# Attention gates of four units moved into the Strassen pairs ahead of attention

## The chip, the cores and the metric

The kernel runs on one core of one Trainium2 chip. The metric is the device time of one execution in microseconds (us); three executions of the kernel before took 1938.79 to 1944.55 us, with a median of 1942.8 us. The engines are TensorE (PE in the profile; its weight loads are PEld), VectorE (DVE), ScalarE (ACT), GpSimd (POOL) and SyncE (SP, which here only issues DMAs).

## The reference

One layer of a hybrid trunk is applied to a prompt of 1024 tokens and to 8 samples of 16 tokens, 1152 tokens in all, with D_MODEL = 1024. One projection feeds everything; only what matters here is kept:

```python
proj = h @ w_in        # columns: q | k | v | z_att | z_ssd | x,B,C | dt | gates
q, k, v, z_att, z_ssd, xbc, dt_raw, gates = jnp.split(proj, IN_SPLITS, axis=-1)
q = rms_norm(q, q_norm_g); k = rms_norm(k, k_norm_g)          # per head of 64
o_att = attn_fn(q, k, v)                                      # chunk band with a bias by distance
att_branch = (o_att * jax.nn.silu(z_att)) @ w_att_proj
...                                                           # SSD branch: y * silu(z_ssd), grouped norm
merged = sigmoid(g_att) * att_branch + sigmoid(g_ssd) * ssd_branch
out = x + gate * (merged @ w_out)
```

The change is about `silu(z_att)`: 1024 columns, that is 8 blocks of 128, one block for each attention unit of two heads.

## The kernel before, in words

Activations lie with channels on partitions, so a block of 128 output columns of the projection is a 128 x 1152 tile. Every projection is done in three fp32r products (high weight by high activation, high by low, low by high; lines 489, 490, 492). Weights are loaded as 128 x 1024 pieces in the order in which the host has packed them ("wall"), into two raw buffers, and split into high and low parts by one ScalarE and one VectorE instruction a piece (`w_split`, lines 374 and 375).

The work comes in this order. (1) Norm and modulation, and the first block: the attention gate of unit 0. (2) The blocks computed ahead (`AHEAD_BLOCKS`, 19 of them): four merge gates singly, then 14 SSD gates as seven Strassen pairs (`pairs`, line 821), then one SSD gate singly. Each result is written to DRAM (`keep_block`), the merge gates to `gate_d` and the SiLU gates to `z_d`; a pair computes two blocks in seven forms of 24 matmuls of 288 columns, where two single blocks are 144 matmuls of 384. (3) Attention, eight units. (4) The SSD branch, 16 pairs of heads, with the remaining merge gates and one SSD gate put between them (`FILL`). (5) The output projections.

One attention unit (`attention`, line 1175) is made of generators. `dense_gen` computes q, k and v token tile by token tile (`dense_tok`, lines 555 to 557: nine tiles of 24 matmuls, with PSUM buffers "d", two of them) and then the SiLU gate of the *next* unit as a plain block (`dense`, 72 matmuls; lines 489, 490, 492, evicted in lines 999 and 1000). `prelude` normalizes q and k on GpSimd (lines 1228 to 1232) in three groups of tiles and transposes them (line 1252 for the first two groups, line 1268 for the third); after the third it frees the q/k buffer. `prompt` and `sample` do the scores (1390, 1443, 1446), the softmax, the transposes of the probabilities (1311), the products with v (1334, 1470, 1480) and multiply by the gate (1395, 1486); when both are through, `done` (line 1289) writes the gated result to `att_d` and frees the buffers of gate and v. So while the tiles of unit u+1 run, the scores of unit u are worked off beside them.

Three buffers matter to the steps below. There is one q/k buffer (tag "Q"): `dense_gen` of unit u+1 waits at `walloc` until `prelude` of unit u has freed it. There are five buffers of tag "T" for gates and v. And the q/k/v weights have two slots of three pieces (`L_W3`), one for the high and one for the low part of one unit; the gate's weights lie elsewhere (`L_WA`).

The order in which the code issues instructions is set by a planner, `run` (line 1108): it steps the dense generator, adds the estimated length of each step to a clock, and steps the other generators when their planned times have come and when a credit, earned by dense work, is positive. If the dense generator has to wait for a buffer, only the others are stepped. The builder (`schedule_with_timeline_sim=True`, line 2196) may then rearrange an engine's instructions by a timeline of its own, except those marked `late`, which stay behind the one before them.

Of the kernel before, what the change touches and what calls it, by code (L numbers as in the profile page):

```python
# [7 lines left out]
F32 = mybir.dt.float32  # L8
# [4 lines left out]
P = 128  # L13
# [15 lines left out]
RW = HALO + NP + NB * (HALO + NS)  # L29
EPS = 1e-6  # L30
AHEAD = 2
NEARLY = 15
SLOTS = (('p', 1), ('p', 3), ('p', 6), ('p', 9), ('p', 11), ('p', 13), ('p', 15))
BLOCKS = [("gate", i) for i in range(4)] + [("z", p) for p in range(NPAIR)] + [("gate", i) for i in range(4, 16)]
AHEAD_BLOCKS = BLOCKS[:4 + NEARLY]
FILL = dict(zip(SLOTS, BLOCKS[4 + NEARLY:]))
NGATE = 4 + NEARLY + len(SLOTS) - NPAIR
NZ = 5
NPR = 7
TH = NT // 2  # L40
MH = TH // 2
BIG = -1e30
# [89 lines left out]
def trunk_kernel(ctx: ExitStack, tc: tile.TileContext, h):  # L132
# [188 lines left out]
    acs_d = drp.tile([32, NT], F32, name="acs_d")  # L321
    eacs_d = drp.tile([32, NT], F32, name="eacs_d")
    gate_d = drp.tile([16, P, NT], F32, name="gate_d")
    z_d = drp.tile([1 + NPAIR, P, NT], F32, name="z_d")

    def rsqrt_small(v):

# [14 lines left out]
    def job(*raw):  # L342
        jobs.append([len(parts) + i for i in range(len(raw))])
        parts.extend(raw)
# [117 lines left out]
    for i in range(NZ + 2 * NPR, nz):  # L462
        job(h["wall"][i])
    jobs_att = [len(jobs)]
    for u in range(NU - 1):
        job(*(h["wall"][nz + 4 * u + i] for i in range(3)))
        job(h["wall"][nz + 4 * u + 3])
    job(*(h["wlast"][i] for i in range(4)))
    jobs_att.append(len(jobs))
    for x in [h["wall"][i] for i in range(nz + 4 * NU - 4, 85)] + [h["watt"][i] for i in range(8)] + [h["wssd"][i] for i in range(16)] \  # L470
            + [h["wout"][i] for i in range(8)]:
        job(x)

    def dense(ops, evict, nk=KT, outs=1, last=False, wide=False, order=(0, 1, 2), other=False, third=False, wkeep=lambda x: x):

        i = widx[0]
        widx[0] += 1
        hi, lo = yield from w_wait(i)  # L480
        if len(jobs[min(i + 1, len(jobs) - 1)]) > 3:
            w_next(i, wkeep)

        def mm(ps, o, g, k, parts=(0, 1)):
            tok = slice(g * G3, (g + 1) * G3)
            wc = slice((k * outs + o) * P, (k * outs + o + 1) * P)
            kh, kl = ops[k]
            if 0 in parts:
                nc.tensor.matmul(ps, hi.r[:, wc], kh.r[:, tok], start=k == 0, stop=False)  # L489
                nc.tensor.matmul(ps, hi.r[:, wc], kl.r[:, tok], start=False, stop=False)  # L490
            if 1 in parts:
                nc.tensor.matmul(ps, lo.r[:, wc], kh.r[:, tok], start=False, stop=k == nk - 1)  # L492

        for o in range(outs):
            if wide or (last and o == outs - 1):
                if wide or other:
                    acc = [pg(G3) for _ in range(3)]
                else:
                    sp = pss.tile([P, 2, 512], F32, tag="s", name=nm("s"))
                    acc = [psd.tile([P, G3], F32, tag="d", name=nm("d")) for _ in range(2)] + [sp[:, 0, :G3]]  # L500
                for k in range(nk):
                    while len(ops) <= k:
                        blocked[0] = "operand"
                        yield None
                    for g in range(3):
                        mm(acc[g], o, g, k)
                        if k == nk - 1:
                            yield from evict(o, g, slice(g * G3, (g + 1) * G3), acc[g]) or ()
                        yield 3 * 162.5
                    if last and o == outs - 1:  # L510
                        for x in ops[k]:
                            x.free()
                    if k == 2 and o == 0:
                        w_next(i, wkeep)
                continue
            for g in order:
                if g == 2 and third:
                    ps = pg(G3)
                elif g == 2 and att_left[0] == 0:
                    ps = pss.tile([P, 2, 512], F32, tag="s", name=nm("s"))[:, 0, :G3]  # L520
                else:
                    ps = psd.tile([P, G3], F32, tag="d", name=nm("d"))
                for k in range(nk):
                    while len(ops) <= k:
                        blocked[0] = "operand"
                        yield None
                    mm(ps, o, g, k)
                    if nk == KT and g == order[-1] and k in (3, 5, 7):
                        w_over(i, k)
                    yield 3 * 162.5  # L530
                yield from evict(o, g, slice(g * G3, (g + 1) * G3), ps) or ()
                if o == 0 and (g == 0 or len(jobs[min(i + 1, len(jobs) - 1)]) > 1):
                    w_next(i, wkeep)
        w_done(i)
# [462 lines left out]
    def ev_z(z, keep=lambda x: x):  # L997
        def ev(o, g, tok, ps):
            keep(nc.scalar.activation(z.ap[:, tok], ps, AF.Tanh, scale=0.5))
            keep(nc.vector.scalar_tensor_tensor(z.ap[:, tok], z.ap[:, tok], 1.0, ps, ALU.add, ALU.mult))  # L1000
        return ev
# [8 lines left out]

    def keep_block(n, z):
        what, i = AHEAD_BLOCKS[n - 1]
        dma(gate_d[i] if what == "gate" else z_d[1 + i], z.ap)

    z = [alloc(L_VT, "T", NT)]
    w_done(0)
# [8 lines left out]
    def do(what, *x):  # L1025
        if what == "first":
            ev_z(z[0], late)(0, x[0], groups[x[0]], first[x[0]])
            if x[0] == 2:
                dma(z_d[0], z[0].ap)
                z[0].free()  # L1030
        elif what == "sum":
            t_sum(*x)
        elif what == "split":
            t_split(*x)
        else:
            o, i, c = small_ops[x[0]]
            if c is None:
                late(nc.scalar.activation(o, i, AF.Copy))
            else:
                late(nc.vector.tensor_scalar(o, i, c, None, ALU.mult))  # L1040
# [134 lines left out]
    def attention(u):  # L1175
# [4 lines left out]
        def dense_gen():  # L1180
            qk = yield from walloc(lay, "Q", 16 * P)
            if u == 0:
                turn = alloc(lay, "T", NT)
                z = zs[0] = alloc(lay, "T", NT)
                dma(z.ap, z_d[0])
                turn.free()
            v = yield from walloc(lay, big, NT)
            nb = yield from walloc(lay, "n", 84)
            st["qk"], st["v"], st["nb"] = qk, v, nb
            if u == NU - 1:  # L1190
                dts["raw"] = yield from walloc(lay, "T", NT)

            def ev(t, ps):

                while t == 8 and "turned" not in st:
                    blocked[0] = "q and k of the first tokens"
                    yield None
                c = qk.ap[:, 2 * (t % 8) * P:2 * (t % 8 + 1) * P]
                nc.scalar.activation(c, ps[:, :2 * P], AF.Copy)
                s = alloc(lay, "q", 2 * P)  # L1200
                nc.scalar.activation(s.ap, ps[:, :2 * P], AF.Square)
                nc.vector.tensor_copy(v.ap[:, t * P:(t + 1) * P], ps[:, 2 * P:NQ])
                if u == NU - 1:
                    nc.vector.tensor_copy(dts["raw"].ap[:, t * 32:(t + 1) * 32], ps[:, NQ:])
                nc.vector.tensor_reduce(nb.ap[:, 4 * t:4 * t + 4], s.ap.rearrange("p (h d) -> p h d", d=HD), mybir.AxisListType.X, ALU.add)  # L1205
                s.free()
                st["n"] = t + 1

            yield from dense_tok(ev)
            dma(h["out_v"][u], v.ap[:, 512:])  # L1210
            if u == NU - 1:
                v_phase("ssd", F32)
                v_open[0] = True
                return
            z = zs[u + 1] = yield from walloc(lay, "Z" if u + 1 == NU - 1 else "T", NT)
            yield from dense(hops, ev_z(z))

        def prelude():
            bias = []
# [392 lines left out]
        dts["t"] = clock[0] + 3000  # L1612


    ngate = [max(4, 4 + NEARLY - NPAIR)]

    def fill_dense(*slot):
        what, i = FILL[slot]
        if what == "gate":
            yield from gate_dense()  # L1620
            return

        def ev(o, g, tok, ps):
            t = yield from walloc(L_SSD, "g", G3)
            nc.scalar.activation(t.ap, ps, AF.Tanh, scale=0.5)
            nc.vector.scalar_tensor_tensor(t.ap, t.ap, 1.0, ps, ALU.add, ALU.mult)
            store(z_d[1 + i][:, tok], t.ap)
            stored(t)

        yield from dense(hops, ev)  # L1630
# [54 lines left out]
    def ssd(p):  # L1685
# [51 lines left out]
        def main():  # L1737
# [101 lines left out]
            for t in me + [xd]:  # L1839
                t.free()  # L1840
            z = alloc(lay, "T", NT)
            dma(z.ap, z_d[1 + p])
            te, tz = clock[0] + 4000, clock[0] + 6500
            yield 3500
            for j in range(3):
# [368 lines left out]
```

## Time and profile before

| | |
|---|---|
| median of three executions | 1942.8 us (1938.79 to 1944.55) |
| profiled execution, its own time | 1943.42 us |
| span of the profile | 1941.6 us |
| granted TensorE clock | 0.999 |
| TensorE busy | 1922.7 us (99%) |
| VectorE busy | 1251.5 us (64%) |
| ScalarE busy | 798.3 us (41%) |

The first number is what is compared later; the profile is of one execution. Busy time of TensorE is that of overlapping matmuls, so a stretch in which it is busy throughout is read by how many matmuls it holds, not by its busy share. Rows of the trace give a start and a length in us from the start of the span, and the line of the kernel.

### The profile page before, as it was taken

The page shows a single profiled execution, that of the slowest core. Times are in us where ns is not written, and L with a number is a line of the kernel's source. Part 1 is how long each engine was busy: PE and PEld are TensorE (multiplying, and loading weights), DVE is VectorE, ACT ScalarE, POOL GpSimd, SP SyncE. Part 2 cuts the span into 40 slices and gives each one's busy share as a digit, 9 for nine tenths or more (in the row PEclk, how much of TensorE's full clock was granted, in tenths as well). Part 3 has the DMA queues.
Part 4 walks back from the last instruction along what each step waited for, and adds up shares of the span by engine and source line. Part 5 has one row for each costly group of instructions (what it writes and reads, how often), then busy time and mean ns, then how long its engine had stood idle before and what let it go on. Part 6 is the DMA issues. An engine that isn't in the chain of part 4 may idle for free.

```text
span 1941.6 us, 35765 instructions
## 1 busy us (share of the span) xinstructions
PE 1922.7 (99%) x14259; PEld 1842.4 (95%) x14259; DVE 1251.5 (64%) x2577; ACT 798.3 (41%) x1639; POOL 339.7 (17%) x615
## 2 busy tenths in 40 slices
PE   7999999999999999999999999999999999999999
PEld 5999999999899998998999999999999999999999
DVE  6756634555556456558597988888885434777732
ACT  7533324444454444545655546465453311111200
POOL 0000003213123131221022343242241300000000
PEclk9999999999999999999999999999999999999999
DMA  8222342343333333423345354554558742331341
GB/s 316 92 81 95 109 173 69 96 129 116 97 117 101 122 116 94 130 82 115 119 132 181 132 162 152 168 173 140 160 192 289 292 144 93 105 105 56 89 143 52
DMA packets 85966, 258.73 MB, mean 133 GB/s; under 512 B 14732, under 2 KB 15768, under 8 KB 85800
## 3 DMA queue, kind: packets, MB, share of 16 engines
q1 hardware_dynamic: 77416, 229.57, 36.5%
q0 software_dynamic: 8384, 26.88, 3.6%
q8 instruction: 112, 1.84, 0.4%
q14 instruction: 54, 0.44, 0.1%
HBM read 202.72 MB, written 53.68 MB: 132 GB/s over the span
## 4 chain that ended last, share of the span: by engine, by line
PE 92%; DVE 3%; DMA 2%; ACT 1%; issue 1%; POOL 0%; SPq 0%; ACTq 0%; DVEq 0%; POOLq 0%
PE d L489 11%; PE d L492 11%; PE d L490 11%; PE d L557 5%; PE d L555 5%; PE d L556 5%; PE s L489 4%; PE s L490 4%; PE s L492 4%; PE g L1311 3%; PE g L1334 3%; PE s L1390 2%; PE g L880 2%; PE g L883 2%; PE g L882 2%; PE g L490 1%
## 5 line engine op out<-in xcount | busy, mean ns | idle before, releaser
L489 PE MATMUL d<-rarena 128*128 128x384 f32 x1288 | 437.7, 340 | 0.0
L492 PE MATMUL d<-rarena 128*128 128x384 f32 x1288 | 434.2, 337 | 0.0
L490 PE MATMUL d<-rarena 128*128 128x384 f32 x1288 | 433.3, 336 | 0.0
L489 PEld LDWEIGHTS d<-rarena 128*128 128x128 f32 x1288 | 242.0, 188 | 4.1 <-issue 2.7
L492 PEld LDWEIGHTS d<-rarena 128*128 128x128 f32 x1288 | 241.9, 188 | 2.2 <-issue 2.0
L490 PEld LDWEIGHTS d<-rarena 128*128 128x128 f32 x1288 | 242.1, 188 | 0.8 <-issue 0.4
L557 PE MATMUL d<-va_att,rarena 128*128 128x384 f32 (+1 forms) x567 | 197.6, 349 | 0.0
L555 PE MATMUL d<-va_att,rarena 128*128 128x384 f32 (+1 forms) x567 | 196.7, 347 | 0.0
L556 PE MATMUL d<-va_att,rarena 128*128 128x384 f32 (+1 forms) x567 | 193.7, 342 | 0.0
L374 ACT ACTIVATE rarena<-arena 128x1024 fp32r<-128x1024 f32 x76 | 80.5, 1059 | 262.9 <-PE s L490 173.9
L489 PE MATMUL s<-rarena 128*128 128x384 f32 x488 | 165.6, 339 | 0.0
L490 PE MATMUL s<-rarena 128*128 128x384 f32 x488 | 164.2, 336 | 0.0
L492 PE MATMUL s<-rarena 128*128 128x384 f32 x488 | 163.3, 335 | 0.0
L1299 ACT ACTIVATE ma_att<-ma_att 128x640 f32<-128x640 f32 (+2 forms) x144 | 101.5, 706 | 135.8 <-DVE ma_att L1408 99.7
L1228 POOL TENSOR_SCALAR ma_att<-ma_att 128x16 f32<-128x16 f32 (+1 forms) x24 | 5.2, 218 | 707.3 <-DVE ma_att L1205 417.2
L557 PEld LDWEIGHTS d<-va_att,rarena 128*128 128x128 f32 x567 | 107.0, 189 | 3.9 <-issue 2.7
L555 PEld LDWEIGHTS d<-va_att,rarena 128*128 128x128 f32 x567 | 106.8, 188 | 2.7 <-issue 1.2
L375 DVE TENSOR_TENSOR rarena<-arena,rarena 128x1024 fp32r<-128x1024 f32 x76 | 93.3, 1227 | 22.6 <-ACT rarena L374 22.6
L556 PEld LDWEIGHTS d<-va_att,rarena 128*128 128x128 f32 x567 | 106.8, 188 | 0.5
L1531 DVE SCALAR_TENSOR_TENSOR ma_att<-ma_att,arena 128x1176 f32<-128x1176 f32 x63 | 93.9, 1491 | 9.4 <-ACT ma_att L1528 8.1
L489 PEld LDWEIGHTS s<-rarena 128*128 128x128 f32 x488 | 91.7, 188 | 1.3 <-issue 1.2
L490 PEld LDWEIGHTS s<-rarena 128*128 128x128 f32 x488 | 91.7, 188 | 0.8 <-issue 0.8
(437 smaller groups left out, 4128.0 us busy)
## 6 DMA issues: line engine op xcount, KB each, us to landing
arena<-in_wall_dram SPq DMA_DIRECT2D x85, 512.0 KB, 3.6
ma_att<-in_kc_dram SPq DMA_DIRECT2D x64, 256.0 KB, 4.3
ma_att<-in_vc_dram SPq DMA_DIRECT2D x64, 256.0 KB, 3.5
ma_att<-acs_d SPq DMA_DIRECT2D x23, 576.0 KB, 6.8
ma_att<-y_d SPq DMA_DIRECT2D x15, 576.0 KB, 6.3
arena<-in_wssd_dram SPq DMA_DIRECT2D x16, 512.0 KB, 4.5
z_d<-va_start SPq DMA_DIRECT2D x13, 576.0 KB, 2.8
ma_att<-eacs_d SPq DMA_DIRECT2D x26, 288.0 KB, 3.9
```

The lines of the kernel that those rows point to most:

```text
L374: keep(nc.scalar.activation(hi.r[:, c], b.ap, AF.Copy))
L375: keep(nc.vector.tensor_tensor(lo.r[:, c], b.ap, hi.ap[:, c], ALU.subtract))
L489: nc.tensor.matmul(ps, hi.r[:, wc], kh.r[:, tok], start=k == 0, stop=False)
L490: nc.tensor.matmul(ps, hi.r[:, wc], kl.r[:, tok], start=False, stop=False)
L492: nc.tensor.matmul(ps, lo.r[:, wc], kh.r[:, tok], start=False, stop=k == nk - 1)
L555: nc.tensor.matmul(ps, kh.r[:, tok], wh, start=j == 0, stop=False)
L556: nc.tensor.matmul(ps, kh.r[:, tok], wl, start=False, stop=False)
L557: nc.tensor.matmul(ps, kl.r[:, tok], wh, start=False, stop=j == KT - 1)
L1299: nc.scalar.activation(p, p, AF.Exp, bias=sm_[:, 4 + e:5 + e], scale=-1.0, accum_out=sm_[:, 6 + e:7 + e])
L1311: nc.tensor.transpose(ps[:, s * P:(s + 1) * P], p[:, (j + s) * P:(j + s + 1) * P], ident)
L1334: late(nc.tensor.matmul(po[e * HD:e * HD + HD, a * P:(a + 1) * P], v.ap[:, vc:vc + HD], x.ap[:, o + i * P:o + (i + 1) * P], start=i == 0, ...
L1531: nc.vector.scalar_tensor_tensor(yc, r.ap[:, j:j + n], w4[:, i, j:j + 1], yc, ALU.mult, ALU.add)
```

## The change

The SiLU gates of attention units 1, 3, 5 and 7 are computed with the blocks ahead of attention, as the first two of now nine Strassen pairs, and written to `att_d`. In attention, the units before them load the gate from there in place of computing it. The gate of unit 0 is now kept in `att_d` too, so `z_d` has a row less. The single block behind the pairs and the blocks filled into the SSD branch are the same as before.

```diff
-NEARLY = 15
+NPR = 9
+UNITS = (1, 3, 5, 7)
-BLOCKS = [("gate", i) for i in range(4)] + [("z", p) for p in range(NPAIR)] + [("gate", i) for i in range(4, 16)]
-AHEAD_BLOCKS = BLOCKS[:4 + NEARLY]
+BLOCKS = [("gate", i) for i in range(4)] + [("unit", u) for u in UNITS] + [("z", p) for p in range(NPAIR)] + [("gate", i) for i in range(4, 16)]
+NAHEAD = 5 + 2 * NPR
+AHEAD_BLOCKS = BLOCKS[:NAHEAD]
...
-NPR = 7
...
+    at = nz
     for u in range(NU - 1):
-        job(*(h["wall"][nz + 4 * u + i] for i in range(3)))
-        job(h["wall"][nz + 4 * u + 3])
+        job(*(h["wall"][at + i] for i in range(3)))
+        at += 3
+        if u + 1 not in UNITS:
+            job(h["wall"][at])
+            at += 1
...
-        dma(gate_d[i] if what == "gate" else z_d[1 + i], z.ap)
+        dma({"gate": gate_d, "z": z_d, "unit": att_d}[what][i], z.ap)
...
             z = zs[u + 1] = yield from walloc(lay, "Z" if u + 1 == NU - 1 else "T", NT)
-            yield from dense(hops, ev_z(z))
+            if u + 1 in UNITS:
+                dma(z.ap, att_d[u + 1])
+            else:
+                yield from dense(hops, ev_z(z))
...
-            first.append(kblock(wi, za + c + P, P))
+            if u + 1 not in UNITS:
+                first.append(kblock(wi, za + c + P, P))
```

More of the change, by code (lines that the diff above doesn't have):

```diff
@@ L31 @@
 AHEAD = 2
-NEARLY = 15
+NPR = 9
+UNITS = (1, 3, 5, 7)
 SLOTS = (('p', 1), ('p', 3), ('p', 6), ('p', 9), ('p', 11), ('p', 13), ('p', 15))
-BLOCKS = [("gate", i) for i in range(4)] + [("z", p) for p in range(NPAIR)] + [("gate", i) for i in range(4, 16)]
-AHEAD_BLOCKS = BLOCKS[:4 + NEARLY]
-FILL = dict(zip(SLOTS, BLOCKS[4 + NEARLY:]))
-NGATE = 4 + NEARLY + len(SLOTS) - NPAIR
+BLOCKS = [("gate", i) for i in range(4)] + [("unit", u) for u in UNITS] + [("z", p) for p in range(NPAIR)] + [("gate", i) for i in range(4, 16)]
+NAHEAD = 5 + 2 * NPR
+AHEAD_BLOCKS = BLOCKS[:NAHEAD]
+FILL = dict(zip(SLOTS, BLOCKS[NAHEAD:]))
+GATES_AHEAD = sum(x[0] == "gate" for x in AHEAD_BLOCKS)
+NGATE = GATES_AHEAD + sum(x[0] == "gate" for x in FILL.values())
 NZ = 5
-NPR = 7
 TH = NT // 2
@@ L323, in trunk_kernel @@
     gate_d = drp.tile([16, P, NT], F32, name="gate_d")
-    z_d = drp.tile([1 + NPAIR, P, NT], F32, name="z_d")
+    z_d = drp.tile([NPAIR, P, NT], F32, name="z_d")
     def rsqrt_small(v):
@@ L464, in trunk_kernel @@
     jobs_att = [len(jobs)]
+    at = nz
     for u in range(NU - 1):
-        job(*(h["wall"][nz + 4 * u + i] for i in range(3)))
-        job(h["wall"][nz + 4 * u + 3])
+        job(*(h["wall"][at + i] for i in range(3)))
[3 more added lines that the diff above has]
+            at += 1
     job(*(h["wlast"][i] for i in range(4)))
     jobs_att.append(len(jobs))
-    for x in [h["wall"][i] for i in range(nz + 4 * NU - 4, 85)] + [h["watt"][i] for i in range(8)] + [h["wssd"][i] for i in range(16)] \
+    for x in [h["wall"][i] for i in range(at, 85)] + [h["watt"][i] for i in range(8)] + [h["wssd"][i] for i in range(16)] \
             + [h["wout"][i] for i in range(8)]:
@@ L1028, in do @@
             if x[0] == 2:
-                dma(z_d[0], z[0].ap)
+                dma(att_d[0], z[0].ap)
                 z[0].free()
@@ L1184, in dense_gen @@
                 z = zs[0] = alloc(lay, "T", NT)
-                dma(z.ap, z_d[0])
+                dma(z.ap, att_d[0])
                 turn.free()
@@ L1612, in dt_gen @@
         dts["t"] = clock[0] + 3000
-    ngate = [max(4, 4 + NEARLY - NPAIR)]
+    ngate = [GATES_AHEAD]
     def fill_dense(*slot):
@@ L1626, in ev @@
             nc.vector.scalar_tensor_tensor(t.ap, t.ap, 1.0, ps, ALU.add, ALU.mult)
-            store(z_d[1 + i][:, tok], t.ap)
+            store(z_d[i][:, tok], t.ap)
             stored(t)
@@ L1841, in main @@
             z = alloc(lay, "T", NT)
-            dma(z.ap, z_d[1 + p])
+            dma(z.ap, z_d[p])
             te, tz = clock[0] + 4000, clock[0] + 6500
@@ L2104 @@
     ga = dt0 + 32
-    first = [kblock(wi, za, P)] + [kblock(wi, (ga if what == "gate" else zs) + i * P, P) for what, i in AHEAD_BLOCKS]
+    first = [kblock(wi, za, P)] + [kblock(wi, {"gate": ga, "z": zs, "unit": za}[what] + i * P, P) for what, i in AHEAD_BLOCKS]
     for u in range(NU):
```

## The prediction

> **What bounds the kernel now.** I read the page first, then the stretches around the change, then the instructions at one seam in order of time.
>
> ```profile
> span 1941.6 us, 35765 instructions
> PE 1922.7 (99%) x14259; PEld 1842.4 (95%) x14259; DVE 1251.5 (64%) x2577; ACT 798.3 (41%) x1639; POOL 339.7 (17%) x615
> ...
> PEclk9999999999999999999999999999999999999999
> ...
> PE 92%; DVE 3%; DMA 2%; ACT 1%; issue 1%; POOL 0%; SPq 0%; ACTq 0%; DVEq 0%; POOLq 0%
> ```
>
> TensorE is busy for 99% of the span at full clock, and 92% of the chain that ended last is its work. So a matmul taken out pays in full as long as TensorE still has something to run in its place. The view by stretches shows where the change falls: the seven pairs, the single block behind them, two units of attention (from one pair of L1268 transposes to the next), and two seams between a unit's q/k/v tiles and the next unit's. Columns are length, then busy time of each engine.
>
> ```profile
> core 0: us, PE busy (x) PEld busy (x) DVE busy (x) ACT busy (x) POOL busy (x), PEclk, DMA share, GB/s
> 102.20:258.95 156.75, 156.75 (x1179) 156.75 (x1178) 92.50 (x161) 49.77 (x97) 0.00 (x0) 1.00 0.30 100
> 258.95:271.43 12.48, 12.48 (x74) 12.48 (x73) 5.96 (x8) 4.63 (x6) 0.00 (x0) 1.00 0.78 289
> 323.20:403.60 80.40, 80.40 (x690) 74.17 (x688) 45.03 (x143) 37.53 (x90) 18.84 (x37) 1.00 0.36 111
> 403.60:484.10 80.50, 80.50 (x690) 74.27 (x689) 45.81 (x143) 37.53 (x90) 18.85 (x37) 1.00 0.36 111
> 309.76:323.16 13.40, 13.40 (x81) 13.33 (x81) 6.57 (x8) 4.60 (x9) 9.46 (x23) 1.00 0.46 144
> 384.54:403.60 19.06, 19.06 (x189) 18.24 (x188) 7.71 (x14) 5.57 (x11) 8.52 (x22) 1.00 0.61 201
> ```
>
> TensorE never rests in any of them, VectorE is under 60% in each and ScalarE under half. Both the place that gains work and the place that loses it are bound by TensorE.
>
> **The change part by part.** *Matmul time.* The stretch 102.20 to 258.95 holds seven pairs: 156.75 / 7 = 22.39 us a pair, or 133.3 ns for each of its 168 matmuls of 288 columns. The stretch 258.95 to 271.43 is exactly one plain block: 12.48 us, 173.3 ns for each of its 72 matmuls of 384 columns. The change adds two pairs (44.8 us) and takes out four plain blocks (49.9 us): **5.1 us less** TensorE work. VectorE in the pairs stands at 92.50 of 156.75 us, so two more pairs run at the same rate.
>
> [...]
>
> *Work of other engines.* Four blocks' evictions, each three ScalarE and three VectorE instructions, leave attention, and the pairs' own evictions go where both engines have room. Nothing on the path.
>
> *Transfers.* Each of the four gates gets a store of 576 KB from the pairs and a load of 576 KB in attention; both queue on SP.
>
> ```profile
> z_d<-va_start SPq DMA_DIRECT2D x13, 576.0 KB, 2.8
> ...
> ma_att<-z_d SPq DMA_DIRECT2D x4, 576.0 KB, 3.9
> ```
>
> The store takes 2.8 us and the load 3.9. The load is issued a whole tile pass ahead of the first product that reads it (`prompt` of the next unit), so it is covered; uncovered it would cost 3.9 us a gate. Its buffer (tag "T") was last used by a unit that ended before this one's tiles did, so I expect SP not to stop on it; behind it stand the weight pieces and the cached keys.
>
> *The seam.* This is where the price lies. For u = 0, 2, 4, 6 the q/k/v tiles of unit u are now followed directly by those of u+1, without the 12.48 us of gate matmuls between. One seam as it is now, TensorE in order of time (start, length, line):
>
> ```profile
> 384.37 0.34 PE L557 MATMUL d<-va_att,rarena 128*128 128x384 f32 x1
> 384.54 0.34 PE L489 MATMUL d<-rarena 128*128 128x384 f32 x1
> ...
> 388.97 3.50 PE L1334 MATMUL g<-ma_att 128*64 128x128 f32 x60
> 392.40 1.30 PE L1470 MATMUL g<-ma_att 128*32 128x128 f32 x40
> ...
> 397.38 0.27 PE L1480 MATMUL g<-arena,ma_att 128*128 128x128 f32 x1
> 397.49 0.60 PE L1252 MATMUL g<-arena,ma_att 128*128 128x128 f32 x4
> ...
> 403.60 0.38 PE L1268 MATMUL g<-arena,ma_att 128*128 128x128 f32 x2
> 403.73 0.42 PE L555 MATMUL d<-va_att,rarena 128*128 128x384 f32 x1
> ```
>
> The tiles end at 384.54, the gate block fills until 403.60, and the next unit's tiles start right behind L1268, which reads the last of the q/k buffer (one slot "Q") that these tiles overwrite. Of the 19.06 us, 12.48 are the gate and 6.6 are attention's. Three things become late without the gate. First, the weights: the q/k/v slots hold one unit's weights, so the next ones can only be split as the old are read out.
>
> ```profile
> 380.69 1.06 ACT L374 ACTIVATE va_att<-arena 128x1024 fp32r<-128x1024 f32 x1 [0.59 <-PE d L557]
> 382.70 1.06 ACT L374 ACTIVATE va_att<-arena 128x1024 fp32r<-128x1024 f32 x1 [0.28 <-PE d L557]
> ...
> 387.31 1.06 ACT L374 ACTIVATE va_att<-arena 128x1024 fp32r<-128x1024 f32 x1 [1.85 <-DMA arena<-in_wall_dram]
> ```
>
> ```profile
> 388.40 2.13 DVE L375 TENSOR_TENSOR va_att<-arena,va_att 128x1024 fp32r<-128x1024 f32 x1 [2.00 <-ACT va_att L374]
> ```
>
> Two of the three pieces are split by the time the tiles end; the third waits for its transfer and is whole at 390.53, 6.0 us after the end. The first two hold five of eight contraction blocks: 15 matmuls, 2.6 us a tile, in each of two PSUM buffers "d". Second, L1268's own input, from GpSimd (unit 0 last):
>
> ```profile
> 393.74 0.61 POOL L1232 TENSOR_TENSOR ma_att<-ma_att 128x256 f32<-128x256 f32 x1
> ```
>
> ```profile
> 319.98 0.61 POOL L1232 TENSOR_TENSOR ma_att<-ma_att 128x256 f32<-128x256 f32 x1
> ```
>
> It is there at 394.35, 9.8 us after the end (unit 0: 320.59, 10.8 us after 309.76), far ahead of 403.60. Only then can the first new tile leave PSUM, some 11 to 12 us after the end. Third, the buffer for the new v is that of the gate of u-1, free once `done` has stored it.
>
> ```profile
> 393.77 0.28 ACT L1476 ACTIVATE ma_att<-g 128x128 f32<-128x128 f32 x1 [4.91 <-PE g L1470]
> ```
>
> ```profile
> 398.17 0.33 SPq L1293 DMA_DIRECT2D att_d<-ma_att  x1
> ```
>
> That store ends about 2.8 us behind its issue, at 401, 16.5 us after the end; L1480 could run from 394.05 and not 397.38, and then it is 13.2. Against that stands what TensorE has on hand: 6.6 us of attention and 2 x 24 x 0.1733 = 8.3 us of two whole tiles, 14.9 us, so a seam is short by 0 to 1.6 us. Unit 0 has no older unit beside it: 13.40 - 12.48 = 0.9 us and 8.3 us against 11.7, short by up to 2.5. I take 1.6 us for unit 0 and 0.6, 0.6 and 0.5 for the others (the last unit's tiles are wider, which is more work on hand): **3.3 us**. This needs the tile matmuls to be placed ahead of waiting transposes. The builder orders an engine's instructions by a timeline of its own, and the trace shows it doing that:
>
> ```profile
> 337.19 0.33 PE L1390 MATMUL g<-rarena 64*128 64x384 f32 x1
> 337.45 0.44 PE L557 MATMUL d<-va_att,rarena 128*128 128x384 f32 x1
> 337.82 0.44 PE L1390 MATMUL g<-rarena 64*128 64x384 f32 x1
> ```
>
> One lone tile matmul (the code issues them in threes) has been put between score matmuls. No gain can hide in the seams: TensorE has no idle time there to lose, so the bounds of this cost are 0 and rival B's 21.1.
>
> **Sum.** The profiled execution took 1943.4 us around its span of 1941.6; 1943.4 - 5.1 + 3.3 = 1941.6. The median of the runs shown, 1942.8, is 0.6 lower, so I forecast **1941.0**, own range 1938.5 to 1944.
>
> **Rivals.** *A, the seams cost nothing:* 1942.8 - 5.1 = 1937.7. For it: the 14.9 us on hand and input ready long before its use. Against it: unit 0's seam, which has no attention to lay over.
>
> *B, the tiles stay behind L1268,* as they stand at 403.73 now. TensorE then idles from the end of its 6.6 us until L1268 is through: 9.8 + 0.4 - 6.6 = 3.6 us at three seams, 10.8 + 0.4 - 0.9 = 10.3 at unit 0, in all 21.1: 1942.8 - 5.1 + 21.1 = 1958.8. For it: that order is what the code writes (`walloc` of "Q" stops the unit's matmuls until the transposes have been issued). Against it: the lone L557 above. It decides if no tile matmul starts ahead of L1268 at a seam. [...]
>
> *C, slower: the queue holds on the third weight piece.* If the timeline that orders TensorE takes the piece for earlier than it lands, tile 0's sixth contraction block stands at the head while other ready work is behind it. TensorE then runs 2.6 us and waits until 6.0: 3.4 us at four seams, 13.6: 1942.8 - 5.1 + 13.6 = 1951.3. For it: the third ACT row waits for its transfer, and the 12.48 us that hid that are gone. Against it: up to 6.6 us of attention lies ahead in the order at three of the seams.
>
> *D, attention's own chain sets a unit's length.* Then units keep their 80.4 us and the added pairs come on top: up to 1942.8 + 44.8 = 1987.6. For it: every unit takes the same 80.4 to 80.5. Against it: TensorE is busy for all of that, with VectorE at 45.81 and ScalarE at 37.53.
>
> **How the numbers follow.** The forecast has 0.44, A 0.25, C 0.13, B 0.10, D 0.04; 0.04 remains for a gain that no row names (a better order further on). About 0.3%, 5.8 us, is what can be told from no change. Faster than 1937.0 needs the lower part of A or the unnamed gain: 0.11. Slower than 1948.6 are most of C, B and D: 0.24. The rest, 0.65, is no change. The range runs from 1936.5, A with the spread of the runs, to 1953, C with the same; outside lie B, D and the unnamed gain.
>
> **What would show each step.** The pairs' stretch should be 9 x 22.4 = 201.5 us long, then one block of 12.48. The first tiles of units 1, 3, 5 and 7 should start 9 to 12 us sooner behind the last of their predecessor, and the distance from L1268 to L1268 fall from 80.4 to about 68 to 71 us where it ends at unit 2, 4 or 6, and stay near 80 at the others. At the seams, L555 rows ahead of L1268 speak for the forecast and a TensorE gap ending at L1268 for B; a gap ending at ACT L374 or DVE L375 for C. In attention as a whole the idle time of TensorE should be 2 to 5 us. The prediction is wrong if that idle time is over 9 us, if a unit without its gate block keeps 80 us, or if the gate's load shows up as what VectorE waits for.

## The result, and the profile after

The changed kernel takes 1947.94 us (median of ten executions, 1945.75 to 1951.19) where the kernel before takes 1943.66 on the same chip (ten, 1938.79 to 1945.85): ratio 1.0024, 95% interval 1.0014 to 1.0034. It is 4.3 us slower. The forecast was 1.8 us faster (1941.0 against 1942.8); the time lies in the wide range that the prediction gave last (1936.5 to 1953), above the forecast's own range (1938.5 to 1944), and on the other side of no change.

The profiled execution took 1947.9 us around this span; the page of the kernel after:

```profile
span 1946.1 us, 35956 instructions
...
PE 1925.9 (99%) x14307; PEld 1837.6 (94%) x14307; DVE 1256.4 (65%) x2609; ACT 802.2 (41%) x1651; POOL 342.9 (18%) x615
...
PEclk9999999999999999999999999999999999999999
...
PE 90%; DVE 3%; DMA 3%; ACT 2%; POOL 1%; issue 1%; SPq 0%; ACTq 0%; POOLq 0%; DVEq 0%
```

It reads as before: TensorE 99% busy at full clock, 90% of the chain. The page can't show what was lost, and the stretches must. First the kernel before, its seven pairs and then attention from the first q/k/v tile to the last product with v (length, then busy time of each engine with its instructions):

```profile
102.35:258.95 156.60, 156.60 (x1178) 156.60 (x1178) 92.50 (x161) 49.77 (x97) 0.00 (x0) 1.00 0.30 100
271.43:956.92 685.49, 685.49 (x5694) 634.36 (x5694) 384.81 (x1189) 314.82 (x753) 155.97 (x313) 1.00 0.34 106
```

The same view of the kernel after: nine pairs, the single block, attention, and then the seam behind unit 0 and two distances from one unit's third transposes (L1277, which was L1268) to the next:

```profile
100.94:302.29 201.35, 201.35 (x1514) 201.35 (x1514) 119.92 (x209) 64.02 (x125) 0.00 (x0) 1.00 0.29 100
302.29:314.77 12.48, 12.48 (x74) 12.48 (x73) 6.01 (x8) 4.63 (x6) 0.00 (x0) 1.00 0.71 250
314.77:962.43 647.66, 645.94 (x5407) 586.54 (x5407) 364.19 (x1173) 304.68 (x737) 156.60 (x313) 1.00 0.35 113
353.10:364.15 11.05, 10.93 (x70) 9.76 (x69) 7.48 (x20) 4.73 (x14) 9.42 (x23) 1.00 0.62 173
364.15:438.50 74.35, 72.97 (x629) 65.67 (x630) 39.95 (x128) 34.88 (x82) 18.80 (x38) 1.00 0.37 117
438.50:513.00 74.50, 74.50 (x657) 67.41 (x656) 45.55 (x153) 36.24 (x93) 18.84 (x37) 1.00 0.35 116
```

The pairs take what was said (44.75 us more for two more of them). Attention is 685.49 - 647.66 = 37.8 us shorter, where four blocks of 12.48 us were taken out. So **12.1 us were lost inside attention**, and only 647.66 - 645.94 = 1.7 us of it is time in which TensorE did nothing. All the waits on other engines that the profile lists for its matmuls there (engine and line, what it waited for: us in all, times, longest) come to less still; in the kernel before the same list is empty:

```profile
PE g L1320 <- DVE ma_att L1324: 0.7, 1, 0.7
PE g L1320 <- ACT ma_att L1285: 0.4, 1, 0.4
PE g L1277 <- POOL ma_att L1241: 0.2, 1, 0.2
```

What is left must be matmuls that take longer than they did. In the table each matmul is given the time from its start to the start of the next one on TensorE, summed over attention by kind (my own sums over the trace's start times, us):

| | before | after |
|---|---|---|
| q/k/v tiles (1728 matmuls) | 321.50 | 323.91 |
| scores (624; L1390, now L1399) | 55.03 | 61.01 |
| transposes of probabilities (560) | 52.17 | 56.53 |
| transposes of q and k (128) | 12.73 | 13.30 |
| products with v, prompt (960) | 55.82 | 55.82 |
| uninterrupted runs of score matmuls | 41 | 63 |

The plain blocks left in the stretch are not in the table: 287 of their matmuls are gone, and 51.6 us with them, 1.8 more than 173.3 ns each. The same number of score matmuls takes 6.0 us more, and they now come in 63 runs and not 41. One such run, at the seam behind unit 0, TensorE and its weight loads in order of time:

```profile
353.80 0.34 PE L562 MATMUL d<-va_att,rarena 128*128 128x384 f32 x1
353.80 0.19 PEld L563 LDWEIGHTS d<-va_att,rarena 128*128 128x128 f32 x1
353.97 0.34 PE L563 MATMUL d<-va_att,rarena 128*128 128x384 f32 x1
354.24 0.19 PEld L1399 LDWEIGHTS s<-rarena 64*128 64x128 f32 x2 [0.25 <-issue]
354.24 0.33 PE L1399 MATMUL s<-rarena 64*128 64x128 f32 x2
...
355.03 0.34 PE L1399 MATMUL s<-rarena 64*128 64x384 f32 x2
355.30 0.19 PEld L561 LDWEIGHTS d<-va_att,rarena 128*128 128x128 f32 x1 [0.25 <-issue]
355.30 0.44 PE L561 MATMUL d<-va_att,rarena 128*128 128x384 f32 x1
```

From one tile matmul to the next the step is 0.17 us, and the next weights are loaded under the running matmul (353.80). From a tile matmul, whose operands have 128 rows, to a score matmul, which has 64, the step is 0.27 us and the load begins only with it; the way back is the same.

### The profile page after: what moved, and what is told of

Read it like the earlier page. It is cut to its first block, busy times and chain, and to the rows that moved or that the text cites. A ratio compares the mean times of both kernels' runs of the same rounds, so it can differ in the third digit from the quotient of the medians.

```text
span 1946.1 us, 35956 instructions
## 1 busy us (share of the span) xinstructions
PE 1925.9 (99%) x14307; PEld 1837.6 (94%) x14307; DVE 1256.4 (65%) x2609; ACT 802.2 (41%) x1651; POOL 342.9 (18%) x615
## 4 chain that ended last, share of the span: by engine, by line
PE 90%; DVE 3%; DMA 3%; ACT 2%; POOL 1%; issue 1%; SPq 0%; ACTq 0%; POOLq 0%; DVEq 0%
PE d L495 10%; PE d L498 10%; PE d L496 10%; PE d L561 5%; PE d L563 5%; PE d L562 5%; PE s L495 4%; PE s L496 4%; PE s L498 4%; PE g L1320 3%; PE g L1343 3%; PE g L886 2%; PE g L889 2%; PE g L888 2%; PE s L1399 2%; PE g L1839 1%
## 5 line engine op out<-in xcount | busy, mean ns | idle before, releaser
L495 PE MATMUL d<-rarena 128*128 128x384 f32 x1192 | 403.9, 339 | 0.0
L498 PE MATMUL d<-rarena 128*128 128x384 f32 x1192 | 402.4, 338 | 0.0
L496 PE MATMUL d<-rarena 128*128 128x384 f32 x1192 | 401.0, 336 | 0.0
L495 PEld LDWEIGHTS d<-rarena 128*128 128x128 f32 x1192 | 224.0, 188 | 2.9 <-issue 1.8
L498 PEld LDWEIGHTS d<-rarena 128*128 128x128 f32 x1192 | 223.9, 188 | 2.6 <-issue 2.0
L496 PEld LDWEIGHTS d<-rarena 128*128 128x128 f32 x1192 | 224.0, 188 | 0.6 <-issue 0.2
L376 ACT ACTIVATE rarena<-arena 128x1024 fp32r<-128x1024 f32 x72 | 76.1, 1058 | 258.5 <-PE s L496 169.8
L377 DVE TENSOR_TENSOR rarena<-arena,rarena 128x1024 fp32r<-128x1024 f32 x72 | 88.6, 1230 | 22.6 <-ACT rarena L376 22.3
```

Of the source, the lines that this page charges most:

```text
L376: keep(nc.scalar.activation(hi.r[:, c], b.ap, AF.Copy))
L377: keep(nc.vector.tensor_tensor(lo.r[:, c], b.ap, hi.ap[:, c], ALU.subtract))
```

## The experiments

Two theories stood against each other. **W**: the seams without a gate block lose time in waits, which are hidden in the records. **O**: the seams are filled, but with matmuls of the next unit and scores in another order; each switch between 128-row and 64-row matmuls costs TensorE time although nobody waits.

### The two halves apart

*Nine pairs, attention as before* (the change without its part in attention):

```diff
-            if u + 1 in UNITS:
-                dma(z.ap, att_d[u + 1])
-            else:
-                yield from dense(hops, ev_z(z))
+            yield from dense(hops, ev_z(z))
...
```

> The ahead part alone: nine pairs are computed and stored, and attention still computes all of its gates as before (the four stored ones are overwritten unused). Costed from the rows: before + 2 x 22.39 = before + 44.8 us. If the two added pairs cost more than that (evictions, splits or stores in the way), it is over before + 48; if the loss lies in attention, within 1.5 us of before + 44.8.

1985.37 us against 1942.61, ratio 1.0219 (1.0205 to 1.0233): 42.8 us more, 2.0 below the 44.8 and so a little outside the 1.5 us allowed, though the interval (39.8 to 45.3) holds 44.8. In its trace the pairs are 44.74 us longer and attention is 685.49 us, as before to the hundredth.

*Seven pairs, four gates not computed* (the four units load unit 0's gate):

```diff
+UNITS = (1, 3, 5, 7)
...
+            if u + 1 in UNITS:
+                dma(z.ap, z_d[0])
+            else:
                 yield from dense(hops, ev_z(z))
...
```

> Attention's part alone: seven pairs as before, the gate blocks of units 1, 3, 5, 7 are left out and the gate of unit 0 is loaded in their place (the output of these units is that of another gate). The prediction's terms give -49.9 + 3.3 = -46.6 us against before. The trace of the changed kernel says that attention became only 37.9 us shorter; if the loss is all in attention, the run is before - 38. With no loss in attention it would be before - 49.9.

1903.03 us, ratio 0.9795 (0.9782 to 0.9809): 39.6 us less. Attention takes 646.88 us, 38.6 less than before. So the loss lies in attention and needs nothing from the pairs: 49.9 us of matmuls taken out bring 38.6, 11.3 us are lost (12.1 in the changed kernel).

### One seam

The same with unit 5's gate alone (`UNITS = (5,)`).

> One seam alone: as the run before it, but only the gate block of unit 5 is left out (the gate of unit 0 stands in for it). Theory O (the order at a seam without a gate block cuts the runs of score matmuls and costs time without a wait): 6 more cuts here against 22 at all four seams, about a quarter of the 12 us, so before - 9.5 to - 10. Theory W (waits for the third weight piece and for the third transposes' input): this seam has older attention to lay over, little is lost, before - 12. Theory that only the seam of unit 0 and the last one cost: before - 12.5.

1930.91 us, ratio 0.9943 (0.993 to 0.9957): 11.7 us less. The time alone decides nothing: it is nearer to W's 12 than to O's 9.5 to 10, and the interval (8.3 to 13.6) holds both. The trace does: attention, which is 685.49 us long in every kernel here that keeps all gates and the planner's order, is 10.23 us shorter, so 2.25 us are lost at one seam in the middle of attention. This profile lists not one wait of a matmul in attention; scores take 1.43 us more and come in 47 runs and not 41. That speaks for O, a loss with no listed wait, and against the third theory, by which only the first and the last seam cost.

### Scores held back

The changed kernel, with the scores issued only behind the unit's third transposes, so that they don't mix with the tiles at the seam:

```diff
+                        st["third"] = nc.tensor.transpose(...)
...
+                            with tc.issue_after(st["third"].ins):
                                 late(nc.tensor.matmul(banks[k][e][:, o:o + w], ...
```

> The changed kernel, and each unit's score matmuls are issued behind its third transposes (L1277) as they were before the change; tile matmuls may still go ahead of them. Theory O: the score runs are cut 53 times and not 63 (41 before the change), so about half of the 6.0 us that the scores cost more comes back, 2 to 4 us less than the changed kernel. Theory W: the waits at the seams stay or grow, same as the changed kernel or slower by up to 3 us.

1948.98 us, ratio 1.0031 (1.0019 to 1.0043): no gain. O's 2 to 4 us didn't come, and the time is what W gave. The score runs fall from 63 to 53 as forecast, but the scores only to 59.78 us, 1.2 less where 3 were expected, and now TensorE waits. The waits of its matmuls in attention, the longest of them:

```profile
PE d L561 <- DVE ma_att L1208: 1.5, 1, 1.5
PE d L562 <- DVE va_att L377: 1.0, 2, 0.9
PE g L1320 <- ACT ma_att L1322: 0.9, 1, 0.9
```

TensorE is idle for 4.7 us of attention, where the changed kernel has 1.7. One loss was exchanged for the other: what mixed with the tiles had been the work that filled the seam.

### Cutting the runs on purpose

The kernel before, with all its gates; only the planner is made to put a step of dense work behind each piece of scores:

```diff
                     cost += 3 * (max(w, 240) / 2.27 + 10)
+                    credit[0] = cost - 1.0
+                    yield cost
+                    cost = 0
                 yield cost
```

> The kernel before the change, all seams with their gate blocks, but the planner is made to put one dense step behind each piece of a round of scores; in the issued order the score matmuls then stand in 70 runs and not 41. No matmul is added or left out. Theory O (a cut in a run of score matmuls costs TensorE time by itself, 0.25 to 0.27 us each by the changed kernel's 22 and the single seam's 6): the scores take 7 to 8 us more, the kernel 5 to 8 us more, without TensorE waits over 2 us. Theory W (the loss at the seams was short waits for weights and GpSimd): same as before, within 2 us.

1955.33 us against 1942.53, ratio 1.0061 (1.0047 to 1.0074): 12.8 us more, above the 5 to 8 that O gave. There are 70 runs of scores and not 41, and again no wait of a matmul is listed in attention. That stretch is 15.65 us longer, 5.6 of it from 32 dense matmuls that moved in from behind; the other 10.1 are order alone, 4.1 on the scores, the rest on the tiles and transposes between them. The 2.7 us that are left lie outside attention and were not followed. W gave no change here, so waits at a seam can't be the whole of it: cuts cost time where no seam was opened. O's sizes missed both ways. The scores' own share is 4.1 us and not 7 to 8 (0.14 us a cut), and the share of the tiles and transposes, 6.0 us, I had left out.

### The price by itself

Behind the end of the kernel before, five stretches of the same 96 matmuls of 128 rows x 384 columns and 96 others, in blocks of n of each kind in turn; nothing waits for another engine:

```diff
+    def mk(i): ... matmul(pd, rbase[:, w], rbase[:, 1024:1408])                  # 128 rows
+    def mq(i): ... matmul(pq[:, e, :256], rbase[hs, w], rbase[hs, 1024:1280])    # 64 rows, halves in turn
+    def mr(i): ... matmul(pq[:, i % 2, 256:512], rbase[:, w], rbase[:, 1024:1280])  # 128 rows
+    for other, n in ((mq, 96), (mq, 12), (mq, 2), (mr, 96), (mr, 2)):
```

> The kernel before, with five short stretches of TensorE work added behind its end, which compute nothing that is used: 96 matmuls of 128 rows x 384 columns and 96 others, put out in blocks of 96, 12 or 2 of each kind in turn. In the first three stretches the others have 64 rows x 256 columns, alternating between the two halves of the rows as the score matmuls do; in the last two (blocks of 96 and of 2) they have 128 rows x 256 columns. No matmul waits for another engine, so a difference between stretches of the same matmuls is the price of their order alone. Theory O (a switch between 128 rows and 64 rows costs TensorE time, since the weight load of the next matmul isn't begun under the one before it): from the traces a tile's step before a score matmul takes 0.268 us in place of 0.174, the second step of a tile behind one takes 0.283 in place of 0.174, so a switch there and back costs 0.2 to 0.35 us; the stretch in blocks of 12 (8 times there and back) is 1.5 to 2.5 us longer than the one in blocks of 96, and the stretch in blocks of 2 (48 times) 9 to 16 us longer. With 128 rows throughout, blocks of 2 take what blocks of 96 take, to 0.5 us. Theory W (the scores lose time only where they wait for a bank of PSUM or for operands): all three 64-row stretches are equal to 0.5 us.

The five stretches in their order, each cut from its first matmul to the next stretch's first:

```profile
1936.80:1959.48 22.68, 22.68 (x193) 22.30 (x193) 0.62 (x1) 0.00 (x0) 0.00 (x0) 1.00 0.03 9
1959.48:1985.03 25.55, 25.55 (x195) 22.48 (x193) 0.00 (x0) 0.00 (x0) 0.00 (x0) 1.00 0.00 1
1985.03:2026.62 41.59, 41.59 (x194) 23.20 (x193) 0.00 (x0) 0.00 (x0) 0.00 (x0) 1.00 0.00 0
2026.62:2054.88 28.26, 28.26 (x195) 28.26 (x193) 0.00 (x0) 0.00 (x0) 0.00 (x0) 1.00 0.00 1
2054.88:2083.25 28.37, 28.37 (x194) 28.27 (x192) 0.00 (x0) 0.00 (x0) 0.00 (x0) 1.00 0.00 1
```

The same 192 matmuls take 22.68 us in blocks of 96, 25.55 in blocks of 12 and 41.59 in blocks of 2. There are 47 more switches there and back in the third than in the first: 18.91 / 47 = **0.40 us each** (2.87 / 7 = 0.41 in the second; both from one execution). With 128 rows on both sides the order makes a difference of 0.11 us (28.26 and 28.37). And note the first column of busy time: TensorE counts as busy for all of the 41.59 us. The weight loads tell more; one switch there and back in the third stretch, then one in the fifth:

```profile
1987.62 0.30 PEld L2071 LDWEIGHTS d<-rarena 128*128 128x128 f32 x2
1987.62 0.62 PE L2071 MATMUL d<-rarena 128*128 128x384 f32 x2
1988.17 0.19 PEld L2076 LDWEIGHTS s<-rarena 64*128 64x128 f32 x2 [0.25 <-issue]
1988.17 0.39 PE L2076 MATMUL s<-rarena 64*128 64x256 f32 x2
1988.48 0.30 PEld L2071 LDWEIGHTS d<-rarena 128*128 128x128 f32 x2
1988.49 0.62 PE L2071 MATMUL d<-rarena 128*128 128x384 f32 x2
```

```profile
2060.19 0.51 PE L2071 MATMUL d<-rarena 128*128 128x384 f32 x2
2060.36 0.36 PEld L2079 LDWEIGHTS s<-rarena 128*128 128x128 f32 x2
2060.54 0.40 PE L2079 MATMUL s<-rarena 128*128 128x256 f32 x2
2060.66 0.31 PEld L2071 LDWEIGHTS d<-rarena 128*128 128x128 f32 x2
```

With 128 rows throughout, the load for the next block begins under the matmul before it (2060.36, and the matmul that uses it at 2060.54). At a change of rows the load and the matmul that uses it start together, with the loader idle for 0.25 us ahead. O is borne out here: a switch costs time, and the next load begins late at it. Its price is a little above the 0.2 to 0.35 us that I had put down, and so are both stretches (2.87 us against 1.5 to 2.5, 18.9 against 9 to 16).

Attention itself gives the same price. In the kernel after, by medians of start-to-start times, a tile matmul ahead of a run of scores takes 0.094 us more than among its like and the first one behind a run 0.107; the first pair of 256-column scores in a run takes 0.104 us more than one inside it, and the last pair 0.090. That is 0.40 us for each run.

### Two middle seams

One pair of attention gates instead of two, priced from the one-seam run: `UNITS = (3, 5)`, `NPR = 8`.

> One more pair in place of two: only the gates of units 3 and 5 are computed ahead (eight pairs), so the two seams without a gate are the middle ones. Theory O prices each such seam by the one-seam run, at 12.49 - 10.23 = 2.26 us lost, and the pair at 22.37: attention 20.4 us shorter than before (665.0), the pairs 22.4 longer, the kernel about 1.9 us slower than before, ratio 1.001, and 3.4 us slower than with one more pair of merge gates; the score matmuls go up by 2 x 1.43 to 57.9 us. Theory W (the loss of the changed kernel is the waits of its first and last seam): attention is 24.5 to 25 us shorter, the kernel 2 us faster than before.

Its attention:

```profile
292.82:957.85 665.03, 665.03 (x5550) 610.45 (x5550) 371.13 (x1181) 309.10 (x745) 156.94 (x313) 1.00 0.33 110
```

665.03 us against 665.0 by O and about 660.8 by W; scores 57.88 against 57.9; the pairs 22.37 longer. The losses of the two middle seams add up, and again no wait is listed. The kernel's time, 1942.89 us against 1941.75 (ratio 1.0002, 0.9993 to 1.0011), is too near to no change to tell 1.9 us slower from none by itself; 2 us faster (0.999) is outside the interval.

### Other blocks in the pairs

Do the prices of pair and block hold where no seam is opened? The kernel before with two pairs more, taken from the merge gates that fill the SSD branch and the stretch ahead of the output projections (`NEARLY = 19`, `NPR = 9`):

> Nine pairs as in the change, but the blocks for the two more pairs are an SSD gate and three merge gates instead of the four attention gates (the last SSD gate and merge gates 4 to 6 go ahead, the SSD fill slots take gates 7 to 13, and two and not six blocks remain between the SSD branch and the output projections). Attention keeps all gate blocks. If the loss is the seams', attention is 685.5 us long as before and the gain of 5.1 us is seen: 5 us less than before. Rival: the blocks ahead of the output projections hid loads and splits, and with two left TensorE waits there; then same or slower.

1965.2 us against 1942.53, ratio 1.0107 (1.0093 to 1.012): 22.7 us more; the rival came, and not the gain. The profiled execution was the shortest of five, 1960.47 us. In it attention is 685.49 us, untouched; behind it, one wait of a matmul stands out, and the chain that ended last has these steps in it (start, length):

```profile
PE g L489 <- ACT rarena L1927: 15.9, 1, 15.9
```

```profile
1504.62 6.34 DMA ma_att<-acs_d
...
1524.42 7.89 DMA va_ssd<-att_d
...
1532.34 1.17 ACT rarena L1927
```

Without those blocks, TensorE stands for 15.9 us at the end of the SSD branch until attention's results have been loaded and split. The granted clock changes with it: from 1520.00, 2.4 us into the wait, to 1537.10, 3.5 us after TensorE has started again, it is one half. In that time a run of 16 matmuls of line 1830 takes 1.91 us on the chain (1534.88), where a later run of 16 takes 1.02 (1539.77). The rest of the wait, then the work behind it (the granted clock is third from the end):

```profile
1520.00:1533.55 13.55, 0.00 (x1) 0.00 (x1) 8.30 (x21) 4.54 (x6) 3.91 (x6) 0.50 1.01 397
1533.55:1537.10 3.55, 3.55 (x20) 2.78 (x21) 1.61 (x2) 1.16 (x1) 0.00 (x0) 0.50 0.51 183
```

And with one pair more (`NEARLY = 17`, `NPR = 8`), which leaves four such blocks there:

> The same with eight pairs: one more pair, four blocks remain ahead of the output projections. If the loss is the seams' alone, 2.6 us less than before; if the blocks left ahead of the output projections are the limit, this one gains and the run with nine pairs does not.

1941.08 us against 1942.53, ratio 0.9992 (0.9982 to 1.0003). In its trace the pairs are 22.37 us longer, attention is 685.49 us and what follows is 980.75 - 956.06 = 24.7 us shorter, where two blocks are 24.96. Here a block pays what it costs. This is the fastest of the kernels tried that compute all of it; that it beats the kernel before isn't settled by these runs.

### The loss against the cuts

"Lost" is what attention fell short of 12.48 us a block taken out (with runs cut on purpose: its 10.1). The fourth column is the number of added runs times 0.40 us; the last is the time in attention in which TensorE was idle.

| kernel | lost, us | added score runs | x 0.40 us | idle, us |
|---|---|---|---|---|
| changed | 12.1 | 22 | 8.8 | 1.7 |
| seven pairs, four gates out | 11.3 | 22 | 8.8 | 1.2 |
| one seam | 2.25 | 6 | 2.4 | 0 |
| two middle seams | 4.5 | 12 | 4.8 | 0 |
| runs cut on purpose | 10.1 | 29 | 11.6 | 0 |
| changed, scores held | 12.5 | 12 | 4.8 | 4.7 |

Cuts and idle time together explain the loss to 0.3 us at the middle seams and leave 1.6 of 12.1 us in the changed kernel; where the runs were cut on purpose they give 1.5 us too much, and the held kernel leaves 3.0 us. What these differences are made of is not shown.

## Why the prediction was wrong

**The pairs, right.** Two pairs at 22.39 us were to cost 44.8 (the stretch read for it began 0.15 us ahead of the first pair; 22.37 is the figure); the trace has 44.75, with VectorE at 119.92 of 201.35 us, and the single block behind them 12.48.

**The blocks, right in price.** 12.48 us a block is what two merge gates brought (24.7 of 24.96).

**Work of other engines and transfers, right.** No instruction waits for the load of a gate. The only wait on `att_d` in attention is VectorE's, for the store of a finished unit, whose buffer the new v takes (the third thing that I had named as late); no matmul waited for it in turn:

```profile
  DVE ma_att L1208: 3.8, 1
```

**Tiles ahead of waiting transposes, right, and further than said.** The first tile of unit 1 starts at 353.10, directly behind the last of unit 0, 13.5 us sooner behind it than before (309.76 to 323.30), and those of units 3, 5 and 7 follow as directly, 19 us sooner; I had said 9 to 12. At the seam of unit 0 the rows that I had named as late come in time:

```profile
356.54 1.06 ACT L376 ACTIVATE va_att<-arena 128x1024 fp32r<-128x1024 f32 x1 [2.51 <-DMA arena<-in_wall_dram]
357.63 2.46 DVE L377 TENSOR_TENSOR va_att<-arena,va_att 128x1024 fp32r<-128x1024 f32 x1 [2.52 <-ACT va_att L376]
...
361.82 1.03 PE L1261 MATMUL g<-arena,ma_att 128*128 128x128 f32 x8
...
363.30 0.78 POOL L1241 TENSOR_TENSOR ma_att<-ma_att 128x256 f32<-128x256 f32 x1
...
364.14 0.44 PE L1277 MATMUL g<-arena,ma_att 128*128 128x128 f32 x2
```

The third weight piece is whole at 360.09, 7.0 us after the tiles' end (forecast 6.0), and the third transposes start 11.0 us after it (forecast: input ready at 10.8). TensorE worked on unit 1's first tiles and on scores until then, idle for 0.1 us.

**The seam's price, wrong: this is the step that failed.** "A seam is short by 0 to 1.6 us", in all "3.3 us", counted only the time in which TensorE would have nothing to do, put the price of a changed order at nothing without a reason, and took the work on hand at the 0.1733 us that a tile matmul takes among its like. As idle time it was about twice too large and not where I had put it: the windows show 1.7 us, 0.8 at unit 0's seam and just behind it (forecast 1.6), none at the two middle ones (0.6 each), 0.2 at the last (0.5), and 0.7 at 423.56, at a seam that keeps its gate block. But the work that fills a seam is laid between scores, the score runs are cut from 41 to 63, and each cut takes 0.40 us of a TensorE that counts as busy. Attention lost 12.1 us, 8.8 more than the term. With it the sum would have been 1943.4 - 5.1 + 12.1 = 1950.4 us against the 1947.9 of the profiled execution; 2.4 of the 2.5 us left over lie outside pairs and attention: the first matmul of the pairs came 1.4 us earlier (100.94 against 102.35), and the part behind attention was 1.0 us shorter. None of the three signs of being wrong that the prediction gave came up, since all of them look for time that TensorE or VectorE spends waiting, or for a unit that keeps 80 us.

I had the row in hand. The lone tile matmul at 337.45, between two scores at 337.19 and 337.82, which I quoted to show that the builder pulls tiles ahead, shows its price too: 0.63 us from score to score.

**The distances, wrong.** From third transposes to third transposes I expected 68 to 71 us where a gate is missing and 80 elsewhere. They are 72.1 to 77.5 throughout, since the tiles of units 1, 3, 5 and 7 now begin 10 to 13 us ahead of the transposes that close the unit before, and that work counts to the distance before; two in the middle make 74.5 + 76.2 = 150.7 us, 2.3 more than 160.9 - 12.5.

**The rivals.** A, seams that cost nothing, fell: idle time was small, as it said, but that isn't all of the cost. B, tiles behind the third transposes, didn't happen. C, a wait of 3.4 us for the third weight piece at four seams, came only as a trace of it (a weight load that waited 0.38 us at 360.15); its 1951.3 was the nearest to the result, by another mechanism. D fell: units became shorter.

## What to carry to other kernels

In this kernel, with TensorE 99% busy, two blocks taken out ahead of the output projections brought 24.7 of 24.96 us, and four taken out of attention, where the order around them changed, 37.8 of 49.9: look at what a block stood between. Count how often TensorE goes between matmuls of different row or column counts, and look at the start-to-start times there (here 0.27 and 0.28 us in place of 0.173), before trusting a sum of matmul times, and remove filler blocks where removing them opens no such mixing. If scores must be held together, something else has to be ready to fill the gap, or the cut is only turned into a wait (4.7 us idle here, in place of 1.7).

## What was not expected of the hardware

In the price run a switch from 128-row to 64-row matmuls and back cost 0.40 us with nothing else in the way, and it doesn't appear as idle time: TensorE's busy row counts it (41.59 of 41.59 us), and only the weight loads show 0.25 us of "issue" ahead of them. From start to start a 128-row matmul takes 0.268 us ahead of a 64-row one and 0.28 us as the first behind one, in place of 0.173 (medians over the stretches of the price run and over attention). It isn't the row count alone: in attention before the change, again by medians, a tile matmul takes the same 0.27 us ahead of the products with v, which have 128 rows and 64 columns of weights, and 0.28 us behind matmuls with 128 rows and 32 columns. The runs of these are 24 and 33, before and after the change, so they are no part of the loss here.

By their shapes, a 128-row load behind a 128-row matmul takes rows that are in use, and begins under it all the same (2060.36, 0.18 us ahead of its own matmul at 2060.54); a 64-row load behind a 128-row matmul takes rows in use too, and begins only with its own matmul (1988.17). So rows in use don't decide it by themselves; what does, no run here shows.
